# Ring of three in-place tiles for gates and z, and the late modulation's columns in the ring of the weights

## The chip, the cores and the metric

One NeuronCore of one Trainium2 chip runs one layer of a diffusion backbone in a single launch. The metric is device time in microseconds, the median of several runs of the whole program. Engines are named as in the profile: PE (TensorE, matmuls), PEld (its weight loads), DVE (VectorE), ACT (ScalarE), POOL (GpSimd), and SP (SyncE), which here only issues transfers.

## The reference, cut to what matters

256 latent tokens and 256 context tokens of width 2048 go through: a modulated RMS norm; one input projection that feeds latent attention (8 heads), a bidirectional gated DeltaNet (8 heads, chunks of 64) and two gates; the merge of both branches with sigmoid gates; one output projection; a second modulated norm; and a gated MLP of hidden width 5504 with a short convolution. Only the latent tokens are returned.

```
sh1, sc1, g1, sh2, sc2, g2 = split(silu(c) @ w_ada + b_ada, 6)
... split_columns(modulate(rmsnorm(x), sh1, sc1) @ w_in)
y_dn = rmsnorm(o, o_norm) * silu(z)
merged = sigmoid(gate_mla) * (y_mla @ w_o_mla) + sigmoid(gate_dn) * (y_dn @ w_o_dn)
x = x + g1 * (merged @ w_out)
x = x + g2 * conv_glu(modulate(rmsnorm(x), sh2, sc2), w_up, conv, w_down)
```

The first two parts of the modulation (`sh1`, `sc1`) are needed at once. The other four (`g1`, `sh2`, `sc2`, `g2`: 8192 columns of `w_ada`, 64 MB) are needed only from the output projection on: they are the late modulation of the title.

## The kernel before

**Layout and staging.** Activations lie transposed, channels on the 128 partitions, tokens along the free dimension (T = 256). Every large weight comes from HBM in pieces of 128 x 1024 f32 (512 KB) into a ring `raw` of NR = 4 slots (L105). `split` (L98 to L101) makes a high part on ACT (`whi`) and the rest on DVE (`wlo`), in halves of 512 columns with NH = 6 buffers each; `mm_hl` (L133) multiplies by the high part with 512 columns and by the low part with 256. So a piece of weights feeds 8 pairs of matmuls.

**Late modulation.** `ada_rest` (L222) goes through 16 blocks of 512 columns. For each it loads 16 tiles of 128 x 512 (256 KB) into a ring `rawa` of NA = 2 slots, one load ahead, and DVE adds each, times one entry of `sc` = silu(c), to `acc` (L238, L240): 256 loads and 256 multiplications in all. Ones-matmuls on PE then sum `acc` over the partitions into `adaT` (L246). It is a generator, driven by a `Side` object: other loops call `ada(ns)`, and it goes on until the budget is used, 650 ns for each step. The loop over DeltaNet heads gives it budget, then the attention, the scan, the output projection and the gated MLP. Before the second norm it is run until 12 blocks are done (L1207).

**Gates and z.** `gate_tiles` (L716) computes the 8 tiles of z (`wz`) and 2 x 16 of the gates (`wgm`, `wgd`) as fill work for PE under the attention and the scan. `gate_fin` (L707) brings a result into a tile `zx` (2 buffers), takes its tanh into a tile `zt` (1 buffer) and stores that to DRAM (L714). For z, `z_fin` (L728) multiplies on DVE first.

**Stages.** First norm and first projections; DeltaNet heads (`dn_head`); `inverse` (L628), a triangular inverse of 32 x 32 blocks that DVE computes in 30 steps (L642, L644), beside the projections `wkva` and `wqa`; then 32 small stores of its result to DRAM (L652 to L660); attention over 4 pairs of heads with z and gates as fill; the scan; merge, output projection, second norm (`h2_tile`, L1218) and gated MLP. At the start of attention the rotated key `krf` is copied to the other partitions by a DMA (L783) and cast to `krt`; `kps`, `ksq` and `ks` are the keys, their squares and their sums.

**What sets the order.** The code is traced in this order, but a list scheduler orders the instructions of each engine by its own estimates, with priority to what was traced first and once a slot is free. Every engine then runs its list in order. All transfers, loads and stores alike, are issued by SP in one list: one that waits for a slot or for data holds up all behind it.

Of the kernel before, what the change touches and what calls it, by code (L numbers as in the profile page):

```python
# [8 lines left out]
F32 = mybir.dt.float32  # L9
F32R = mybir.dt.float32r  # L10
AF = mybir.ActivationFunctionType
ALU = mybir.AluOpType
# [4 lines left out]
P = 128  # L17
D = 2048
KD = D // P
T = 256  # L20
# [6 lines left out]
G3 = 96 + 256 * N1  # L27
GR = 1024
GH = 512
NR = 4  # L30
NA = 2
NH = 6
AD = 0.45
GD0 = 2
# [20 lines left out]
def hybrid_block(ctx: ExitStack, tc: tile.TileContext, io, dbg=None):  # L55
    nc = tc.nc
    act, dve, pool, pe, sync = nc.scalar, nc.vector, nc.gpsimd, nc.tensor, nc.sync


    def pool_(name, bufs, side="left"):  # L60
        return tc.tile_pool(name=name, bufs=bufs, side=side, reuse_waits="tile")

    const = ctx.enter_context(pool_("const", 1))
    ad = ctx.enter_context(pool_("ad", 2))
    hp = ctx.enter_context(pool_("hp", 1))
    wr = ctx.enter_context(pool_("wr", 2))
# [17 lines left out]
    def vectors(pl, name, names):  # L84
        t = pl.tile([P, io[name].shape[1]], F32, name=name)
        sync.dma_start(t, io[name])
        pos, d = 0, {}
        for nm, n in names:
            d[nm] = t[:, pos : pos + n]
            pos += n  # L90
        return d

    off = vectors(const, "vecs", VECS)
# [9 lines left out]
    def raw_w(src):  # L103
        n = src.shape[1]
        raw = wr.tile([P, GR], F32, tag="raw", name="raw", bufs=NR)[:, :n]  # L105
        sync.dma_start(raw, src)
# [37 lines left out]
    def col_sum(out, x, w, start=True, stop=True):  # L144

        for j in range(4):
            js = slice(32 * j, 32 * j + 32)
            pe.matmul(out[js], x[:, js], w, start=start, stop=stop)
# [73 lines left out]
    def ada_rest():  # L222

        def load(i):
            w = ad.tile([P, 512], F32, tag="rawa", name="rawa", bufs=NA)
            b, q = divmod(i, 16)
            sync.dma_start(w, io["wada2"][b, q // 4, :, q % 4 * 512 : q % 4 * 512 + 512])
            return w

        ahead = [load(i) for i in range(NA - 1)]  # L230
        for b in range(16):
            acc = ad.tile([P, 512], F32, tag="acc", name="acc")
            for q in range(16):
                if 16 * b + q + NA - 1 < 256:
                    ahead.append(load(16 * b + q + NA - 1))
                w, c = ahead.pop(0), sc[:, q, 0:1]
                if q == 0:
                    dve.tensor_scalar(out=acc, in0=w, scalar1=c, scalar2=None, op0=ALU.mult)  # L238
                else:
                    dve.scalar_tensor_tensor(out=acc, in0=w, scalar=c, in1=acc, op0=ALU.mult, op1=ALU.add)  # L240
                if q < 15:
                    yield 650
            ps = psa.tile([P, 4], F32, tag="aux", name="adp")
            for j in range(4):
                col_sum(ps[:, j : j + 1], acc[:, j * P : (j + 1) * P], ones[:, 0:1])
            dve.tensor_tensor(out=adaT[:, 4 * b : 4 * b + 4], in0=ps, in1=bada[:, 32 + 4 * b : 36 + 4 * b], op=ALU.add)  # L246
            ada.done = b + 1
            yield 650
# [22 lines left out]
    sc = const.tile([P, KD, 2], F32, name="sc")  # L271
# [20 lines left out]
    def shift_mm(p):  # L292
# [3 lines left out]
        for m in range(4):  # L296
            raw = wr.tile([P, GR], F32, tag="raw", name="raw", bufs=NR)
            sync.dma_start(raw, io["wadab"][p, m])
# [79 lines left out]
    def gather(ps, M, out, scale=None):  # L378

        act.copy(out, ps[:M, T:])  # L380
        dve.tensor_tensor(out=out, in0=ps[:M, :T], in1=out, op=ALU.add)
# [49 lines left out]
    u = pg.tile([P, 8, 8], F32, name="ux")  # L431
# [48 lines left out]
    for st in range(8):  # L480
        B = [pg2.tile([P, 8, 64], F32R, tag=f"B{n}", name="B") for n in range(2)]
        for n in range(2):
            dve.tensor_tensor(out=B[n], in0=mle64.unsqueeze(1).broadcast_to([P, 8, 64]),
                              in1=ghl[:, n, st].unsqueeze(2).broadcast_to([P, 8, 64]), op=ALU.mult)
# [114 lines left out]
    def head_inputs(h):  # L599
# [13 lines left out]
        return xs[0], xs[1], xq  # L613

    ada = Side(ada_rest())
    ada.done = 0
    order = (0, 3, 1, 4, 2, 5, 6, 7)
# [84 lines left out]
    Ys = dram.tile([P, HEADS, T], F32, name="Ys")  # L702
    Zs = dram.tile([P, HEADS, T], F32, name="Zs")
    Gs = dram.tile([2, P, KD, T], F32, name="Gs")
    pz = ctx.enter_context(pool_("pz", 2))

    def gate_fin(ps, out, fin):  # L707
        x = pz.tile([P, T], F32, tag="zx", name="zx")
        gather(ps, P, x)
        t = pz.tile([P, T], F32, tag="zt", name="zt", bufs=1)  # L710
        act.activation(t, x, AF.Tanh, scale=0.5)
        if fin is not None:
            fin(x, t)
        sync.dma_start(out, t)  # L714

    def gate_tiles(jobs):  # L716

        for w, f, out, fin in jobs:
            W = lazy_w(io[w][f])
            ps = psm.tile([P, 512], F32, tag="mm", name="gtp")  # L720
            for k in range(KD):
                mm_hl(ps, P, W(k * P), H[0][:, k], k == 0, k == KD - 1)
                if k % 4 == 3 and k < KD - 1:
                    yield 1300
            gate_fin(ps, out, fin)
            yield 1300

    def z_fin(x, t):  # L728
        dve.scalar_tensor_tensor(out=t, in0=t, scalar=1.0, in1=x, op0=ALU.add, op1=ALU.mult)
        dve.tensor_scalar(out=t, in0=t, scalar1=off["o_norm"], scalar2=0.5, op0=ALU.mult, op1=ALU.mult)  # L730

    fill = Side(gate_tiles([("wz", f, Zs[:, f], z_fin) for f in range(HEADS)] + [("wgm", f, Gs[0, :, f], None) for f in range(KD)]))
    pC = ctx.enter_context(ExitStack())
    pc = pC.enter_context(pool_("pc", 1))
# [248 lines left out]
    for b in range(4):  # L983
        at, pr = mla_attend(b), mla_project(b + 1) if b < 3 else iter(())
        for n in range(7):
            for st in (pr, at):
                c = next(st, None)
# [256 lines left out]
    for f in range(NFF):  # L1244
        xs = []
        for w in ("wgate", "wval"):
# [6 lines left out]
            x = pf2.tile([P, T], F32, tag=w, name="fx")  # L1253
# [121 lines left out]
```

## Time and profile before

| | |
|---|---|
| three runs, median (lowest to highest) | 1940.28 us (1939.37 to 1945.17) |
| profiled execution: its time, its span | 1937.21 us, 1935.4 us |
| mean granted TensorE clock | 0.967 |
| DMA traffic over the span | 418.26 MB, mean 216 GB/s |
| share of the span with PE busy, DVE busy, ACT busy | 94%, 74%, 47% |

The span runs from the first to the last instruction of the profiled execution. Engine shares are averages over stages that are limited by different things, so the views by stretch of time, by waits and by line count for more. A wait in these views is idle time of an engine, put down to what ended it. In the prediction, 0 is the start of the span, and a line such as L240 is a line of the kernel before.

### The profile page before, as it was taken

To read this page: it belongs to the slowest core of one execution; us is meant where nothing else is said; L and a number is where in the kernel's file an instruction comes from. 1 tells how busy PE (TensorE), PEld (TensorE's weight loads), DVE (VectorE), ACT (ScalarE), POOL (GpSimd) and SP (SyncE) were. 2 spreads that over 40 slices of the span, in tenths; PEclk is the share of its full clock that TensorE was granted. 3 is DMA by queue.
4 is the path that set the end of the run, shared out by engine and by line. 5 is a ranking of instruction groups with operands and counts; after the bars stand their busy time and mean duration, and the time that the engine had idled before them with its cause. 6 is when DMAs were issued, how large, how long until landed. Compare 5 with 4: busy or idle time off the path is not lost.

```text
span 1935.4 us, 34978 instructions
## 1 busy us (share of the span) xinstructions
PE 1826.2 (94%) x13186; PEld 1552.7 (80%) x13186; DVE 1437.0 (74%) x2854; ACT 915.9 (47%) x1882; POOL 41.7 (2%) x45
## 2 busy tenths in 40 slices
PE   7889988999879999999999997999999999999999
PEld 5677867788678878778888885888888888888887
DVE  4998887777768778656679888887778777755554
ACT  3224443333367656543245545555554555544443
POOL 0000000000000000000000000000000000000000
PEclk7899988999889999999999998999999999999999
DMA  8984576665676777788776886776667565566664
GB/s 319 317 290 163 170 202 204 202 195 183 124 239 209 221 223 227 239 254 260 227 266 206 259 282 201 251 252 184 189 203 236 186 184 186 179 195 200 194 193 128
DMA packets 222521, 418.26 MB, mean 216 GB/s; under 512 B 71504, under 2 KB 113616, under 8 KB 219920
## 3 DMA queue, kind: packets, MB, share of 16 engines
q1 hardware_dynamic: 222352, 416.04, 69.1%
q8 instruction: 103, 1.69, 0.4%
q14 instruction: 66, 0.54, 0.1%
HBM read 387.00 MB, written 28.84 MB: 215 GB/s over the span
## 4 chain that ended last, share of the span: by engine, by line
PE 50%; issue 10%; DMA 6%; DVE 4%; ACT 1%; POOL 0%; SPq 0%; POOLq 0%; DVEq 0%; ACTq 0%
PE fps L141 13%; PE dps L141 8%; PE fps L142 7%; DMA rawa<-in_wada 5%; PE gtp L141 5%; PE dps L142 4%; PE gtp L142 2%; DVE acc L240 1%; DVE wlo L101 1%; PE brp L141 1%; PE kp L1084 1%; PE fps L139 1%; PE yp L1093 1%; DMA raw<-in_wgate 1%; PE op L1105 1%
## 5 line engine op out<-in xcount | busy, mean ns | idle before, releaser
L101 DVE TENSOR_TENSOR wlo<-raw,whi 128x512 fp32r<-128x512 f32 (+1 forms) x940 | 634.9, 685 | 197.4 <-ACT whi L100 186.2
L100 ACT CAST whi<-raw 128x512 fp32r<-128x512 f32 (+1 forms) x940 | 571.7, 618 | 415.5 <-PE dps L141 117.4
L141 PE MATMUL fps<-H,whi 128*128 128x512 f32 x1290 | 461.9, 399 | 5.8 <-DVE H L101 5.8
L142 PE MATMUL fps<-H,wlo 128*128 128x256 f32 x1290 | 363.7, 282 | 2.4 <-DVE wlo L101 2.4
L141 PEld LDWEIGHTS fps<-H,whi 128*128 128x128 f32 x1290 | 243.3, 189 | 62.3 <-DVE H L101 4.8
L142 PEld LDWEIGHTS fps<-H,wlo 128*128 128x128 f32 x1290 | 244.8, 190 | 7.7 <-DVE wlo L101 4.0
L240 DVE SCALAR_TENSOR_TENSOR acc<-rawa,sc,acc 128x512 f32<-128x512 f32 x240 | 179.2, 747 | 76.7 <-DMA rawa<-in_wada 75.4
L141 PE MATMUL mmp<-h,whi 128*128 128x512 f32 x600 | 225.2, 413 | 0.9 <-ACT whi L100 0.9
L141 PE MATMUL gtp<-h,whi 128*128 128x512 f32 x600 | 220.8, 404 | 0.0
L141 PE MATMUL dps<-GB,whi 128*128 128x512 f32 x544 | 193.0, 397 | 0.0
L142 PE MATMUL mmp<-h,wlo 128*128 128x256 f32 x600 | 174.8, 292 | 7.7 <-DVE wlo L101 7.7
L142 PE MATMUL gtp<-h,wlo 128*128 128x256 f32 x600 | 171.0, 285 | 0.0
L142 PE MATMUL dps<-GB,wlo 128*128 128x256 f32 x544 | 153.1, 282 | 0.0
L141 PEld LDWEIGHTS mmp<-h,whi 128*128 128x128 f32 x600 | 117.5, 196 | 27.7 <-ACT whi L100 1.3
L141 PEld LDWEIGHTS gtp<-h,whi 128*128 128x128 f32 x600 | 113.6, 189 | 25.8 <-issue 1.5
L142 PEld LDWEIGHTS mmp<-h,wlo 128*128 128x128 f32 x600 | 118.1, 197 | 10.2 <-DVE wlo L101 8.4
L141 PEld LDWEIGHTS dps<-GB,whi 128*128 128x128 f32 x544 | 102.1, 188 | 25.3
L142 PEld LDWEIGHTS gtp<-h,wlo 128*128 128x128 f32 x600 | 114.2, 190 | 4.2 <-issue 1.0
L142 PEld LDWEIGHTS dps<-GB,wlo 128*128 128x128 f32 x544 | 102.5, 188 | 0.0
L344 PE MATMUL fp<-h,gh 128*128 128x256 f32 (+1 forms) x224 | 60.9, 306 | 17.0 <-ACT h L335 17.0
L319 DVE CUSTOM_DVE_ANT_0 junk<-wt,scb 128x2048 bf16<-128x2048 f32 x32 | 73.1, 2284 | 0.1
L345 PE MATMUL fp<-h,gh 128*128 128x256 f32 (+1 forms) x224 | 65.9, 302 | 1.6 <-DVE h L336 1.4
(599 smaller groups left out, 2960.5 us busy)
## 6 DMA issues: line engine op xcount, KB each, us to landing
rawa<-in_wada SPq DMA_DIRECT2D x256, 256.0 KB, 4.0
raw<-in_wgate SPq DMA_DIRECT2D x82, 512.0 KB, 4.5
raw<-in_wval SPq DMA_DIRECT2D x82, 512.0 KB, 4.4
raw<-in_wdown SPq DMA_DIRECT2D x80, 512.0 KB, 4.3
wt<-in_wadas SPq DMA_DIRECT2D x16, 1024.0 KB, 7.4
raw<-in_wadab SPq DMA_DIRECT2D x32, 512.0 KB, 6.4
raw<-in_wgm SPq DMA_DIRECT2D x32, 512.0 KB, 4.7
raw<-in_wgd SPq DMA_DIRECT2D x32, 512.0 KB, 5.2
```

The costliest lines, as they stand in the source:

```text
L100: act.copy(hi, raw)
L101: dve.tensor_tensor(out=lo, in0=raw, in1=hi, op=ALU.subtract)
L139: pe.matmul(ps[:M, :], hi, xf, start=False, stop=True)
L141: pe.matmul(ps[:M, :], hi, xf, start=first, stop=False)
L142: pe.matmul(ps[:M, :T], lo, x[:, 0, :], start=False, stop=last)
L240: dve.scalar_tensor_tensor(out=acc, in0=w, scalar=c, in1=acc, op0=ALU.mult, op1=ALU.add)
L319: dve.tensor_tensor_reduce(out=junk, in0=w, in1=scb[:, s], scale=1.0, scalar=0.0, op0=ALU.mult, op1=ALU.add, accum_out=m[:, s : s + 1])
L344: pe.matmul(ps, hi, H[s][:, k, 0], start=k == 0 and s == 0, stop=False)
L345: pe.matmul(ps, hi, H[s][:, k, 1], start=False, stop=False)
L1084: pe.matmul(kp[hs, j], kt[:, h, hs], S[:, h, d], start=True, stop=True)
L1093: pe.matmul(yp[:, j], tt[:, 4 * q + j], rs[q][:, j], start=True, stop=True)
L1105: pe.matmul(op[q][:, j, d], S[:, h, d], qe[:, h, 64 * d : 64 * d + 64], start=False, stop=d == 1)
```

## The change

The tiles of the late modulation take slots of the ring `raw`, which has five now in place of four; the ring `rawa` is gone. A load brings 1024 columns, that is two of the former tiles, and DVE multiplies its halves one after the other; one load is issued ahead as before. A step of `ada_rest` still is one multiplication. The space is the same: four slots of 4 KB and two of 2 KB for each partition became five of 4 KB.

For gates and z, `zx` has three buffers and `zt` none of its own. The tanh of a gate is written over its input; for z the tanh takes a second tile of the same ring, and the product is written over the input. What is stored is `zx`.

```diff
-NR = 4
-NA = 2
+NR = 5
...
         def load(i):
-            w = ad.tile([P, 512], F32, tag="rawa", name="rawa", bufs=NA)
-            b, q = divmod(i, 16)
-            sync.dma_start(w, io["wada2"][b, q // 4, :, q % 4 * 512 : q % 4 * 512 + 512])
+            w = wr.tile([P, GR], F32, tag="raw", name="rawa", bufs=NR)
+            b, u = divmod(i, 8)
+            sync.dma_start(w, io["wada2"][b, u // 2, :, u % 2 * GR : u % 2 * GR + GR])
             return w
 
-        ahead = [load(i) for i in range(NA - 1)]
+        ahead = load(0)
         for b in range(16):
             acc = ad.tile([P, 512], F32, tag="acc", name="acc")
-            for q in range(16):
-                if 16 * b + q + NA - 1 < 256:
-                    ahead.append(load(16 * b + q + NA - 1))
-                w, c = ahead.pop(0), sc[:, q, 0:1]
-                if q == 0:
-                    dve.tensor_scalar(out=acc, in0=w, scalar1=c, scalar2=None, op0=ALU.mult)
-                else:
-                    dve.scalar_tensor_tensor(out=acc, in0=w, scalar=c, in1=acc, op0=ALU.mult, op1=ALU.add)
-                if q < 15:
-                    yield 650
+            for u in range(8):
+                w = ahead
+                if 8 * b + u < 127:
+                    ahead = load(8 * b + u + 1)
+                for q in range(2):
+                    c, wq = sc[:, 2 * u + q, 0:1], w[:, q * 512 : q * 512 + 512]
+                    if u + q == 0:
+                        dve.tensor_scalar(out=acc, in0=wq, scalar1=c, scalar2=None, op0=ALU.mult)
+                    else:
+                        dve.scalar_tensor_tensor(out=acc, in0=wq, scalar=c, in1=acc, op0=ALU.mult, op1=ALU.add)
+                    if u + q < 8:
+                        yield 650
...
-    pz = ctx.enter_context(pool_("pz", 2))
+    pz = ctx.enter_context(pool_("pz", 3))
 
     def gate_fin(ps, out, fin):
         x = pz.tile([P, T], F32, tag="zx", name="zx")
         gather(ps, P, x)
-        t = pz.tile([P, T], F32, tag="zt", name="zt", bufs=1)
-        act.activation(t, x, AF.Tanh, scale=0.5)
-        if fin is not None:
-            fin(x, t)
-        sync.dma_start(out, t)
+        if fin is None:
+            act.activation(x, x, AF.Tanh, scale=0.5)
+        else:
+            fin(x)
+        sync.dma_start(out, x)
...
-    def z_fin(x, t):
-        dve.scalar_tensor_tensor(out=t, in0=t, scalar=1.0, in1=x, op0=ALU.add, op1=ALU.mult)
-        dve.tensor_scalar(out=t, in0=t, scalar1=off["o_norm"], scalar2=0.5, op0=ALU.mult, op1=ALU.mult)
+    def z_fin(x):
+        t = pz.tile([P, T], F32, tag="zx", name="zt")
+        act.activation(t, x, AF.Tanh, scale=0.5)
+        dve.scalar_tensor_tensor(out=x, in0=t, scalar=1.0, in1=x, op0=ALU.add, op1=ALU.mult)
+        dve.tensor_scalar(out=x, in0=x, scalar1=off["o_norm"], scalar2=0.5, op0=ALU.mult, op1=ALU.mult)
```

**What moves.** Slots that come free at other times make the scheduler order the instructions differently. In the changed kernel line numbers of the same code are one lower up to the function `ada_rest`, one higher behind it, and three higher behind `z_fin`.

DVE in the middle of the inverse, before (`ux` holds the blocks of the inverse, `acc<-rawa` is a multiplication of the late modulation, `kvx` a result of `wkva`):

```order
L644 TENSOR_TENSOR ux<-ux 128x2x11x20
L240 SCALAR_TENSOR_TENSOR acc<-rawa,sc,acc 128x512
L642 TENSOR_TENSOR ux<-ux 128x456
L101 TENSOR_TENSOR wlo<-raw,whi 128x512
L644 TENSOR_TENSOR ux<-ux 128x2x12x19
L240 SCALAR_TENSOR_TENSOR acc<-rawa,sc,acc 128x512
L642 TENSOR_TENSOR ux<-ux 128x468
L240 SCALAR_TENSOR_TENSOR acc<-rawa,sc,acc 128x512
L644 TENSOR_TENSOR ux<-ux 128x2x13x18
```

The same steps of the inverse on DVE now:

```order
L645 TENSOR_TENSOR ux<-ux 128x2x11x20
L100 TENSOR_TENSOR wlo<-raw,whi 128x512
L643 TENSOR_TENSOR ux<-ux 128x456
L645 TENSOR_TENSOR ux<-ux 128x2x12x19
L100 TENSOR_TENSOR wlo<-raw,whi 128x512
L643 TENSOR_TENSOR ux<-ux 128x468
L645 TENSOR_TENSOR ux<-ux 128x2x13x18
```

No multiplication of the late modulation stands within the inverse now, where there were 7 from its first to its last step; of the splits of weights 18 stand there, where there were 23.

SP at the end of the burst of small stores, before (the last four stores of the inverse's result, L653 to L660, and what follows; `wz`, `wkvb` and `wqb` are weights of z and of the attention):

```order
L653 DMA Xd<-ux 32x32x32
L658 DMA Xs<-ux 16x32x32 x4
L660 DMA Xs<-ux 32x16x32 x2
L714 DMA Zs<-zt 128x256
L783 DMA krf<-krf 64x512
L677 DMA xd<-Xd 128x2x128
L106 DMA raw<-in_wkvb 128x1024
L106 DMA raw<-in_wz 128x1024
L714 DMA Zs<-zt 128x256
```

The same place on SP now:

```order
L654 DMA Xd<-ux 32x32x32
L659 DMA Xs<-ux 16x32x32 x4
L661 DMA Xs<-ux 32x16x32 x2
L715 DMA Zs<-zx 128x256
L786 DMA krf<-krf 64x512
L105 DMA raw<-in_wz 128x1024
L678 DMA xd<-Xd 128x2x128
L226 DMA rawa<-in_wada 128x1024
L105 DMA raw<-in_wz 128x1024
L226 DMA rawa<-in_wada 128x1024
L105 DMA raw<-in_wkvb 128x1024
```

Ahead of the burst stand, after the first load of `wkvb`, three loads of `wz` before and one now; the other two and two loads of the modulation stand between `krf` and the second load of `wkvb`.

DVE at the second norm, before (`x` is the sum of input and mixer, `bc_ps` its inverse root mean square, `h` and `H` the normed tiles and their low parts):

```order
L1220 TENSOR_TENSOR h_13567<-bc_ps,x_12429 128x256
L1220 TENSOR_TENSOR h_13580<-bc_ps,x_12429 128x256
L246 TENSOR_TENSOR adaT<-adp,vecs 128x4
L240 SCALAR_TENSOR_TENSOR acc<-rawa,sc,acc 128x512
L101 TENSOR_TENSOR H_13538<-h_13567,H_13538 128x256
L101 TENSOR_TENSOR H_13538<-h_13580,H_13538 128x256
L1220 TENSOR_TENSOR h_13593<-bc_ps,x_12429 128x256
L1220 TENSOR_TENSOR h_13606<-bc_ps,x_12429 128x256
L240 SCALAR_TENSOR_TENSOR acc<-rawa,sc,acc 128x512 x2
L101 TENSOR_TENSOR H_13538<-h_13593,H_13538 128x256
```

The same steps on DVE now:

```order
L1223 TENSOR_TENSOR h_13343<-bc_ps,x_12227 128x256
L1223 TENSOR_TENSOR h_13356<-bc_ps,x_12227 128x256
L100 TENSOR_TENSOR H_13314<-h_13343,H_13314 128x256
L100 TENSOR_TENSOR H_13314<-h_13356,H_13314 128x256
L1223 TENSOR_TENSOR h_13369<-bc_ps,x_12227 128x256
L1223 TENSOR_TENSOR h_13382<-bc_ps,x_12227 128x256
L100 TENSOR_TENSOR H_13314<-h_13369,H_13314 128x256
```

Between the last `x1` and the first result of the gated MLP 14 multiplications stood on DVE, and two stand there now; the two that stood between `x` and the sum of squares (L1200 and L1204) are gone. In the scan there are 34 instead of 17, and behind the second norm 59 instead of 36.

## The prediction

> **What bounds the kernel now.** I read the page first: how much of the span TensorE (PE) is busy, and what its chain holds.
>
> ```profile
> span 1935.4 us, 34978 instructions
> PE 1826.2 (94%) x13186; PEld 1552.7 (80%) x13186; DVE 1437.0 (74%) x2854; ACT 915.9 (47%) x1882; POOL 41.7 (2%) x45
> PE 50%; issue 10%; DMA 6%; DVE 4%; ACT 1%; POOL 0%; SPq 0%; POOLq 0%; DVEq 0%; ACTq 0%
> ```
>
> PE is the bound over the whole: 109 us of the span (1935.4 - 1826.2) are not PE. Matmul work does not change here, so a gain can only come out of those 109 us and out of matmuls that run at a lowered clock behind a gap. An average over stages says little, so the second view is busy time by stretch.
>
> ```profile
> core 0: us, PE busy (x) PEld busy (x) DVE busy (x) ACT busy (x) POOL busy (x), PEclk, DMA share, GB/s
> 446.00:508.00 62.00, 53.39 (x434) 45.06 (x433) 54.97 (x114) 24.33 (x50) 2.34 (x3) 0.86 0.47 141
> 508.00:530.00 22.00, 21.32 (x155) 17.27 (x154) 12.80 (x32) 8.58 (x18) 0.81 (x1) 1.00 0.79 118
> 530.00:546.00 16.00, 4.92 (x81) 4.35 (x80) 6.23 (x14) 6.66 (x13) 1.33 (x1) 0.59 0.89 236
> 546.00:800.00 254.00, 243.68 (x1899) 210.86 (x1898) 198.18 (x421) 161.80 (x378) 12.66 (x11) 0.99 0.72 222
> 1066.00:1178.00 112.00, 108.58 (x668) 92.69 (x666) 95.10 (x183) 55.61 (x118) 0.00 (x0) 1.00 0.82 265
> 1178.00:1217.00 39.00, 25.18 (x171) 20.51 (x164) 31.74 (x72) 22.66 (x49) 0.70 (x1) 0.82 0.65 203
> ```
>
> The first two columns are the stretch and its length. Three stretches lose most: 446 to 508 (the triangular inverse on VectorE, DVE, which is busy 55 of 62 us), 530 to 546 (PE nearly still, clock 0.59) and 1178 to 1217 (the second norm, PE busy 25 of 39). Between 546 and 800 PE loses 10 of 254.
>
> Third, what the modulation costs. Its loads are the largest DMA wait of DVE; the two lower rows give the median from issue to landing of a load of each size.
>
> ```profile
> DVE acc L240 <- DMA rawa<-in_wada: 75.4, 78, 3.0
> rawa<-in_wada SPq DMA_DIRECT2D x256, 256.0 KB, 4.0
> raw<-in_wgate SPq DMA_DIRECT2D x82, 512.0 KB, 4.5
> ```
>
> 75 us over 78 waits, but DVE is not the bound everywhere: such a wait counts only where PE waits behind it.
>
> **The change, part by part.** *Arithmetic:* the 256 multiplications of the modulation stay, on the same shape; two tanh forms and the two z operations stay too. Nothing is priced there. 128 DMA issues fewer on SP's queue, and a load of double size lands in about 4.5 instead of 4.0 us, so two multiplications wait for 4.5 where they waited for 8. That this is hidden or not is settled stage by stage.
>
> *Inverse and the store burst (446 to 546).* This chain carries most.
>
> ```profile
> 446.35 0.21 DVE L642 TENSOR_TENSOR ux<-ux 128x60 f32<-128x60 f32 x1
> 505.93 0.27 DVE L644 TENSOR_TENSOR ux<-ux 128x60 f32<-128x60 f32 x1
> 509.32 0.33 SPq L652 DMA_DIRECT2D Xd<-xt  x1
> 534.60 0.54 SPq L783 DMA_DIRECT2D krf<-krf  x1
> 536.31 0.42 ACT L711 ACTIVATE zt<-zx 128x256 f32<-128x256 f32 x1 [8.27 <-DMA Zs<-zt]
> 536.92 0.62 ACT L100 CAST krt<-krf 128x512 fp32r<-128x512 f32 x1 [0.20 <-DMA krf<-krf]
> 541.52 0.61 PE L148 MATMUL ks<-ones,ksq 128*32 128x1 f32 x32 [11.08 <-ACT ksq L827]
> ```
>
> DVE works through the inverse from 446 to 506; the 32 stores of X follow on SP from 509 to 534; the small stores and `krf` stand behind them. PE's longest gap, 11.08 us, is at the end of this. The ring of three takes away the 8.27 us for which the single `zt` buffer held ScalarE (ACT) until its store had landed. **It gives almost nothing here:** the cast of `krt` is next but one on ACT in the changed order too, and it waits for `krf`, issued at 534.60. In the row it became free 0.20 us after the tanh. So I price that edit at 0 to 0.2 us.
>
> What does move the end of that chain is the DVE work inside the inverse.
>
> ```profile
> L101 DVE TENSOR_TENSOR wlo<-raw,whi 128x512 fp32r<-128x512 f32 x23 | 15.7, 685 | 0.0
> L240 DVE SCALAR_TENSOR_TENSOR acc<-rawa,sc,acc 128x512 f32<-128x512 f32 x7 | 5.2, 747 | 3.4 <-DMA rawa<-in_wada 3.4
> 526.05 0.40 PE L141 MATMUL gtp<-h,whi 128*128 128x512 f32 x1
> 526.41 0.40 PE L141 MATMUL gtp<-h,whi 128*128 128x512 f32 x1
> ```
>
> Seven multiplications stand in it, 5.2 us with 3.4 us of waiting; in the changed order none does. Five of its 23 weight splits fall behind its end: 5 x 0.685 = 3.4 us. Together 5.2 + 3.4 + 3.4 = 12.0 us by which the stores can start earlier. Against it: two loads of `wz` that stood ahead of the burst now stand behind it on SP. Each feeds 8 pairs of matmuls, and a pair takes 0.35 to 0.36 us (526.05 to 526.41): 2 x 8 x 0.35 = 5.6 us of PE work that can no longer fill the burst. The split work that falls behind the inverse goes into the burst, where DVE is busy 13 of 22 us. Net 12.0 - 5.6 = **-6.4 us**; bounds -12.0 (PE finds other work) and +5.6 (the inverse ends no sooner).
>
> *The late attention (546 to 800).*
>
> ```profile
> PE rps L896 <- ACT qx L863: 4.6, 3, 2.9
> DVE acc L240 <- DMA rawa<-in_wada: 31.3, 34, 3.0
> 701.31 0.75 DVE L240 SCALAR_TENSOR_TENSOR acc<-rawa,sc,acc 128x512 f32<-128x512 f32 x1 [2.70 <-DMA rawa<-in_wada]
> 704.42 1.22 PE L896 MATMUL rps<-qx,rope 128*128 128x256 f32 x2 [2.90 <-ACT qx L863]
> ```
>
> DVE waits 31.3 us for these loads, but PE loses only 254.00 - 243.68 = 10.3 us, the 4.6 of the first row included. The two last rows are one event: 2.70 us on DVE become 2.90 us on PE, since DVE finishes `qx` behind the wait. With half the loads I take away half of the 31.3, and of PE's 10.3 I take 4: **-4 us**, bounds 0 and -10.3. DVE's other saving is hidden by the fill matmuls of `wz` and `wgm`; where PE has no idle time, it is worth nothing.
>
> *The second norm (1178 to 1217).*
>
> ```profile
> PE ss L148 <- DVE ssq L1204: 6.3, 1, 6.3
> PE fps L141 <- DVE H L101: 5.8, 5, 2.3
> L240 DVE SCALAR_TENSOR_TENSOR acc<-rawa,sc,acc x13: 739/751/753, 1183.2 to 1217.8; 128x512 f32<-128x512 f32 x13
> 1183.17 0.75 DVE L240 SCALAR_TENSOR_TENSOR acc<-rawa,sc,acc 128x512 f32<-128x512 f32 x1
> ```
>
> DVE makes the tiles of H on which PE waits, and 13 multiplications stand between them (13 x 0.75 = 9.8 us); in the changed order there are two. Those between `x1` and `ssq` cost at most one 0.75 plus one 0.48, partly under the square on ACT. I take 3.3 of the 5.8 and 0.7 of the 6.3: **-4 us**; bounds 0 and -7 (5.8 + 1.2).
>
> *The last loads (1440 to 1500) and the rest.*
>
> ```profile
> PE fps L142 <- DVE wlo L101: 1.8, 2, 1.1
> ```
>
> These 1.8 us stand behind waits for the modulation; its work is spread over more of the gated MLP now: **-1 us**, bounds -3 and +3, the upper for the scan (800 to 1000), which gets 34 multiplications instead of 17. DVE has room there (139 of 216 us busy from 800 to 1016 on the same view), and PE waits for little. From 1300 on PE is full. A weight load feeds 8 pairs, 2.8 us. If the modulation holds two of the five slots, three are left, a round of 8.4 us, in which a load lands (4.5 us) and is split twice (1.4 us on DVE, and the casts before it); so I price that at nothing. Without that cover each late load costs its lateness.
>
> *A rule weighed.* Row first: the granted clock from 530 to 546 is 0.59. The Trainium skill, page "TensorE: Matmul & The Clock Gate", section "Part 1: The HAM clock gate", says that an idle window of about 3.4 us halves the clock and about as long a busy stretch restores it. By that rule a gap that shrinks but stays above 3.4 us saves none of the ramp. Both large gaps stay above it in my sum, so I add nothing; had they gone below it, an estimate from the page's 3.4 us at half speed is 1.7 us more for each, and the sum would be 3.4 us lower. The trace agrees with the rule's direction.
>
> **Sum.** -6.4 - 4 - 4 - 1 = -15.4 us. The profiled execution took 1937.21 us (span 1935.4), so it would take 1921.8. The runs shown have their median at 1940.28, 3.07 above it: 1924.9, say **1925 us**.
>
> **The rivals.** *No change:* the stall moves only. For it: `krf` is late next, the stores of X also wait for ACT and PE, and in 546 to 800 PE is busy 96%. If the inverse gains just the 5.6 us that the two loads cost, and half of the other terms is hidden, the time is 1940 - 4 = 1936, within 5.8 us (0.3%, about what a measurement of this kernel can tell from no change). Against it: DVE's 12 us are on a serial chain that SP waits for.
>
> *Slower, by the shared queue:* behind the burst the second `wkvb` load, which stood third after `Zs`, stands behind two loads of `wz` and two of the modulation. SP issues in order, so one modulation load that waits for a slot holds the attention's weights. Four loads of 0.5 MB at 236 GB/s (530 to 546) are 2.2 us each, 9 us in all. That decides once the inverse ends less than 9 us earlier: with +9 there and the other terms at 0 the time is 1949. Against it: PE has 16 pairs of `gtp` to do meanwhile, 5.6 us.
>
> *Larger:* if DVE really paced 546 to 800, all 10.3 us of PE go and the inverse gives its 12.0: -12 - 10.3 - 7 - 3 = -32, 1908.
>
> *It doesn't do what it says:* the ring of three frees nothing as priced above; this is in the forecast already.
>
> **Chances.** Forecast, 1914 to 1934: 0.62. Larger: 0.11. No change: 0.15. Slower: 0.12. So faster by over 0.3% is 0.73, within it 0.15, slower 0.12. The range is 1908 to 1941: the low end is the sum of the bounds, the high one takes in no change and leaves out most of the slower case.
>
> **What would show it.** The first store of X about 12 us sooner after the first row of the inverse; the gap before `ks` still there and above 3.4 us, ended by `krf` or the `wz` load and no longer by a `Zs` store; DVE's waits for `rawa` near half of 75 us; the waits for H between 1178 and 1217 at half. Wrong would be: weights (`whi` on ACT) waiting for DMA in the attention, or SP held for modulation slots longer than now.

## The result, and the profile after

The changed kernel takes **1919.19 us** (median of 6 runs, 1911.35 to 1928.57) where the kernel before takes 1940.88 (6 runs): a ratio of 0.990, 95% interval 0.988 to 0.992. It is faster, inside the range and 5.8 us below the forecast. The profiled executions differ by 14.7 us (1937.21 and 1922.51; forecast 15.4). The profiled run of before lies 3.7 us below its median and that of the changed kernel 3.3 us above its own, so the medians are further apart than the traces; the traces tell where some 15 us went. (A few executions of the experiments were in a slow state, the first profiled one without waits among them, at a granted clock of 0.60; the ratios leave them out and no trace of one is read.)

The page of the changed kernel, the same rows as before:

```profile
span 1920.4 us, 34673 instructions
PE 1820.5 (95%) x13186; PEld 1550.8 (81%) x13186; DVE 1438.2 (75%) x2854; ACT 922.1 (48%) x1882; POOL 43.1 (2%) x45
PE 76%; issue 10%; DVE 8%; DMA 3%; ACT 1%; SPq 1%; POOL 1%; POOLq 0%; ACTq 0%; DVEq 0%
```

TensorE (PE) works 5.7 us less and idles 9.3 us less (1935.4 - 1826.2 = 109.2, now 1920.4 - 1820.5 = 99.9). The matmul count is the same and the mean granted clock is 0.970 where it was 0.967, so the matmuls took less time because they ran at a higher clock.

For a ledger I cut both traces at the same events: the first `U` of DeltaNet, first and last step of the inverse (446.35 and 505.93 before), first `ks`, first matmul of the scan, its last update of the state (`sp_`), first and last `ops` of the output projection, first `fps` of the gated MLP, and its last part. Busy time by stretch, the kernel before (columns as in the prediction):

```profile
226.70:446.35 219.65, 201.59 (x1746) 167.76 (x1745) 170.77 (x354) 85.82 (x177) 14.19 (x14) 0.93 0.71 205
446.35:505.93 59.58, 50.97 (x420) 42.95 (x419) 53.66 (x111) 22.62 (x48) 2.34 (x3) 0.86 0.46 135
505.93:541.52 35.59, 23.83 (x169) 19.21 (x167) 16.94 (x41) 13.12 (x26) 0.81 (x1) 0.88 0.81 152
541.52:827.70 286.18, 275.10 (x2176) 238.29 (x2176) 214.10 (x448) 179.31 (x411) 16.73 (x15) 0.98 0.74 227
...
965.90:1081.80 115.90, 113.56 (x794) 96.79 (x793) 100.57 (x230) 61.00 (x131) 2.90 (x1) 0.99 0.73 235
1081.80:1177.30 95.50, 92.08 (x545) 78.50 (x543) 78.73 (x146) 45.51 (x95) 0.00 (x0) 1.00 0.83 270
1177.30:1190.50 13.20, 2.89 (x86) 1.95 (x84) 9.44 (x25) 4.24 (x10) 0.70 (x1) 0.66 0.58 188
1190.50:1688.30 497.80, 491.87 (x2849) 425.21 (x2850) 389.70 (x760) 270.47 (x541) 0.00 (x0) 1.00 0.65 205
```

The same view of the changed kernel, cut at the same events:

```profile
231.90:448.00 216.10, 194.22 (x1731) 161.46 (x1732) 168.32 (x350) 87.25 (x180) 15.04 (x14) 0.95 0.70 207
448.00:498.60 50.60, 47.49 (x420) 39.98 (x419) 47.25 (x100) 22.22 (x48) 2.32 (x3) 0.98 0.33 102
498.60:540.00 41.40, 29.26 (x181) 23.36 (x180) 22.08 (x49) 15.43 (x29) 0.69 (x1) 0.82 0.82 178
540.00:813.90 273.90, 271.84 (x2193) 236.84 (x2192) 211.72 (x445) 181.56 (x414) 17.31 (x15) 1.00 0.75 235
...
952.00:1071.30 119.30, 114.52 (x795) 97.13 (x794) 100.94 (x230) 62.25 (x133) 2.89 (x1) 0.99 0.69 227
1071.30:1167.40 96.10, 93.07 (x545) 80.65 (x543) 74.44 (x139) 48.39 (x97) 0.00 (x0) 0.96 0.75 247
1167.40:1176.30 8.90, 1.98 (x54) 1.24 (x52) 4.81 (x16) 3.00 (x7) 0.69 (x1) 0.75 0.29 90
1176.30:1673.20 496.90, 493.54 (x2880) 427.42 (x2881) 398.55 (x777) 273.83 (x541) 0.00 (x0) 0.99 0.67 214
```

Length after minus length before:

| stretch | change, us | in the forecast |
|---|---|---|
| start and DeltaNet, up to the inverse | +5.2 - 3.5 = +1.7 | 0 |
| the inverse | -9.0 | -12.0 |
| from its end to the first `ks` | +5.8 | +5.6 |
| attention, up to the scan | -12.3 | -4 |
| scan; from its end to the first `ops`; `ops` | -0.1; +3.4; +0.6 | 0 |
| second norm | -4.3 | -4 |
| gated MLP | -0.9 | -1 |
| sum | -15.1 | -15.4 |

The sum agrees; the rows for the inverse, the attention and the parts that I had at 0 do not. The waits that answer to those of the prediction, over the whole changed kernel and then in the attention alone (before: 75.4 us in 78 waits, and 31.3 in 34):

```profile
DVE acc L241 <- DMA rawa<-in_wada: 32.7, 28, 5.8
...
DVE acc L241 <- DMA rawa<-in_wada: 8.4, 11, 1.8
...
PE rps L899 <- ACT qx L866: 1.3, 2, 0.9
```

The first is a little under half, as forecast; in the attention they fell by 23 us, far more than half. The 4.6 us of `rps`, the wait of 2.90 us among them, are down to 1.3 us.

### The profile page after: what moved, and what is told of

It reads as the page before. It is cut to its first block, busy times and chain, and to the rows that moved or that the text cites. A ratio compares the mean times of both kernels' runs of the same rounds, so it can differ in the third digit from the quotient of the medians.

```text
span 1920.4 us, 34673 instructions
## 1 busy us (share of the span) xinstructions
PE 1820.5 (95%) x13186; PEld 1550.8 (81%) x13186; DVE 1438.2 (75%) x2854; ACT 922.1 (48%) x1882; POOL 43.1 (2%) x45
## 4 chain that ended last, share of the span: by engine, by line
PE 76%; issue 10%; DVE 8%; DMA 3%; ACT 1%; SPq 1%; POOL 1%; POOLq 0%; ACTq 0%; DVEq 0%
PE fps L140 16%; PE dps L140 8%; PE fps L141 8%; PE gtp L140 6%; PE mmp L140 6%; PE dps L141 4%; PE gtp L141 3%; PE mmp L141 3%; DVE junk L320 3%; PE brp L140 1%; PE fps L138 1%; PE fp L346 1%; PE kp L1087 1%; PE fp L345 1%; PE fp L347 1%
## 5 line engine op out<-in xcount | busy, mean ns | idle before, releaser
L140 PE MATMUL mmp<-h,whi 128*128 128x512 f32 x600 | 217.2, 401 | 2.7 <-ACT whi L99 2.7
L241 DVE SCALAR_TENSOR_TENSOR acc<-rawa,sc,acc 128x512 f32<-128x512 f32 x240 | 179.1, 746 | 34.6 <-DMA rawa<-in_wada 32.7
L141 PE MATMUL mmp<-h,wlo 128*128 128x256 f32 x600 | 170.5, 286 | 7.9 <-DVE wlo L100 7.9
L140 PEld LDWEIGHTS mmp<-h,whi 128*128 128x128 f32 x600 | 113.3, 189 | 27.9 <-ACT whi L99 3.0
L141 PEld LDWEIGHTS mmp<-h,wlo 128*128 128x128 f32 x600 | 113.8, 190 | 11.3 <-DVE wlo L100 9.6
```

Source lines behind the costliest of these rows:

```text
L140: pe.matmul(ps[:M, :], hi, xf, start=first, stop=False)
L141: pe.matmul(ps[:M, :T], lo, x[:, 0, :], start=False, stop=last)
L241: dve.scalar_tensor_tensor(out=acc, in0=wq, scalar=c, in1=acc, op0=ALU.mult, op1=ALU.add)
```

## The experiments

All times are medians; the ratio is to the kernel before, run beside it on the same chip (its medians there: 1940.21, 1938.46 and 1938.74 us). VectorE is DVE, SyncE is SP, ScalarE is ACT, GpSimd is POOL.

| kernel | modulation's loads | weight slots | us | ratio, 95% interval |
|---|---|---|---|---|
| before | 512, own ring of 2 | 4 | 1940 | 1 |
| changed | 1024, shared | 5 shared | 1919.2 | 0.988 to 0.992 |
| ring of three alone | 512, own 2 | 4 | 1943.6 | 1.0001 to 1.003 |
| modulation alone | 1024, shared | 5 shared | 1922.5 | 0.989 to 0.994 |
| shared, 512 | 512, shared | 5 shared | 1937.3 | 0.996 to 0.999 |
| own ring, 1024 | 1024, own 2 | 3 | 1938.0 | 0.996 to 1.0004 |
| three slots | 512, own 2 | 3 | 1959.8 | 1.008 to 1.013 |
| four shared slots | 1024, shared | 4 shared | 1953.7 | 1.005 to 1.009 |
| own ring, 512 deep | 512, own 4 | 3 | 1922.2 | 0.989 to 0.994 |

### One part alone

The ring of three on the kernel before (the hunks at `pz`, `gate_fin` and `z_fin` alone).

> The kernel before with only the ring of three in place for the gate and z tiles; the modulation as before (own ring of two 512-wide tiles, four weight slots). Theory (the prediction): 0 to -0.2 us, ratio 0.999 to 1.001, since the cast of krt waits for krf next; the gap before ks stays at 10 to 11 us and is ended through krf. Rival (the ring of three frees ScalarE): the gap shrinks by up to 8.3 us, ratio near 0.996.

Ratio 1.002, interval 1.0001 to 1.003: nothing gained. Here is ScalarE ahead of the attention in this kernel (start, duration, instruction, and in brackets the idle time before it and what ended it):

```profile
527.37 0.42 ACT L730 ACTIVATE zt<-zx 128x256 f32<-128x256 f32 x1 [0.49 <-DVE zx L381]
536.75 0.62 ACT L100 CAST krt<-krf 128x512 fp32r<-128x512 f32 x1 [8.96 <-DMA krf<-krf]
```

The tanh runs 9 us sooner than before (536.31 there); the 8.27 us wait for the store of `zt` is gone, and 8.96 us for `krf` stand in its place. The step of the prediction is seen in two rows. That PE's gap was 14.19 us here, and not 10 to 11, is the expectation's miss: it ended with a late `wkvb` load.

The other part alone, which is the changed kernel with the old gate and z tiles:

> The changed kernel with the gate and z tiles as before (two zx, one zt): only the modulation's columns go through the ring of the weights, five slots, 1024 per load. Theory: all of the gain, 1919 to 1925 us, ratio 0.988 to 0.992. Rival (the ring of three has a part of it): 1927 to 1933, ratio 0.993 to 0.996.

0.991, interval 0.989 to 0.994, beside 0.988 to 0.992 with both parts: the whole gain within the error. The profiled execution has the same ledger: 239.2 us from the first `ks` to the last `s_` (239.4 in the changed kernel), inverse 50.6 in both.

### Load size, ring or slot

```
-            w = ad.tile([P, 512], F32, tag="rawa", name="rawa", bufs=NA)
+            w = wr.tile([P, GR], F32, tag="raw", name="rawa", bufs=NR)[:, :512]
```

> The kernel before with the modulation's loads left at 512 wide (256 loads) but put into the ring of the weights, five slots. No multiplication stands in the inverse now, as in the changed kernel. Theory (width halves the waits): only the inverse's term is left, -6 us, ratio near 0.997; VectorE still waits about 75 us for rawa. Rival (sharing the ring does it: it moves the multiplications and shortens no load): -15 to -20 us, ratio 0.990 to 0.992.

0.998: the inverse's term and no more, as expected. The inverse takes 50.8 us in its trace, as in the changed kernel, with no multiplication in it. DVE's waits for `rawa` are 57 us, nearer to 75 than to 33. Its attention up to the scan takes 289.8 us, no less than before (286.2). (Its profiled execution is its fastest, 15 us under its median, so I read no total from it.) So sharing the ring moves the multiplications, and that alone is worth about 3 us (1 to 8 by the interval).

The reverse, 1024 per load in a ring of its own; only three weight slots fit beside it:

```
-            w = wr.tile([P, GR], F32, tag="raw", name="rawa", bufs=NR)
+            w = ad.tile([P, GR], F32, tag="rawa", name="rawa", bufs=2)
```

> The modulation's loads 1024 wide (128 loads) in a ring of their own with two tiles; to fit in memory the weights keep three slots. Gate and z tiles as before. Eight multiplications stand in the inverse. Theory (width): the terms of the late attention and the second norm are left, -8 us, less what the lost weight slot costs (0 to 8): ratio 0.996 to 1.000, and VectorE's waits for rawa near 38 us. Rival (sharing the ring does it): nothing gained, ratio 1.000 to 1.005, by the lost slot.

0.998 again, at the middle of the theory's range; waits for `rawa` 32.5 us. The attention up to the scan takes 272.7 us (273.9 in the changed kernel): that gain does not need the shared ring. But the scan takes 150.9 us and not 138.2. To price the lost slot by itself, the kernel before with `NR = 3`:

> The kernel before with three weight slots in place of four and nothing else: the price of a weight slot, which the own ring of 1024-wide tiles had to give up. Theory (that price swallowed the own ring's gain): 8 to 15 us slower, ratio 1.004 to 1.008, most of it in the scan (800 to 970), where the own ring lost 12.7 us. Rival (the slot is free, a wide load on its own gains nothing): ratio 1.000 to 1.002.

1959.8 us, 1.010: some 20 us, above both ranges, and not mainly in the scan (+5.2 there); the output projection has +8.1 and the gated MLP +7.8. Against this kernel the 1024-wide ring gains 1959.8 - 1938.0 = 22 us at equal weight slots, but with 4 KB more of memory per partition for the modulation.

Then the slot count in the shared ring, the modulation alone with `NR = 4`:

> The modulation alone through the ring of the weights at 1024 per load, as in the changed kernel, but with four slots and not five (gate and z tiles as before). Theory: a modulation tile takes the fourth slot most of the time, so this pays about what the loss of a weight slot costs: 1925 to 1935 us, ratio 0.992 to 0.998. Rival (the fifth slot does nothing): 1920 to 1924, ratio 0.989 to 0.992.

1953.7 us, 31 us slower than with five slots and slower than before. Both guesses were too kind. Here the waits of DVE for `rawa` are back at 68 us, and the scan takes 155.6 us. The prediction's "nothing" for the ring holds for five slots and would have been wrong for four.

### How much the waits cost at most

The kernel before with its loads, but the multiplications read a tile that never changes:

```
+        fixed = ident.unsqueeze(1).broadcast_to([P, 4, P])
...
-                    dve.scalar_tensor_tensor(out=acc, in0=w, scalar=c, in1=acc, op0=ALU.mult, op1=ALU.add)
+                    dve.scalar_tensor_tensor(out=acc.rearrange("p (a b) -> p a b", a=4), in0=fixed, scalar=c, in1=acc.rearrange("p (a b) -> p a b", a=4), op0=ALU.mult, op1=ALU.add)
```

> The kernel before with all its loads of the modulation, but the multiplications read one fixed tile, so VectorE never waits for rawa (the modulation's values are not the reference's); two multiplications stand in the inverse, not seven. It bounds what the 75 us of waits cost. Theory (the waits pace the late attention, more than the 4 us that the prediction took): 20 to 30 us faster, ratio 0.985 to 0.990, the stretch from the first ks to the last s_ 14 us shorter or more. Rival (PE hides the waits and the gain is the queue's): the inverse's term and little else, 5 to 8 us, ratio 0.996 to 0.998.

> The kernel whose modulation multiplies a fixed tile while its loads go on, once more, for a profile of it at full clock: its first profile was taken at a granted clock of 0.60, and its time was 43 us below before. Theory (the waits pace every stage that interleaves the modulation with weight splits): the gain is spread, 5 us or more each in DeltaNet (227 to 446), the late attention, wout with the second norm, and the gated MLP. Rival (the late attention alone): 25 us or more of it between the first ks and the last s_.

1896.89 us: 0.978, interval 0.976 to 0.980, more than either theory said. The second run (one execution, 1897.22 us) gave the trace. Its DeltaNet stage, from the first `U` to the inverse:

```profile
224.10:418.80 194.70, 190.78 (x1740) 159.65 (x1741) 170.56 (x352) 85.44 (x176) 13.60 (x14) 1.00 0.82 237
```

219.65 us before, 194.70 here, the clock at 1.00 where it was 0.93: 25 of the 40 us that the traces differ by lie in a stage for which the prediction had no term. The output projection with the second norm gives 10.7 (95.5 + 13.2 before, 89.2 + 8.8 here), the gated MLP 4.2 and the attention up to the scan only 2. Two stretches are longer than before: the one from the inverse to the first `ks` by 10.5 us and the scan by 12.4. They and the attention in this kernel:

```profile
470.10:516.20 46.10, 31.72 (x177) 25.65 (x175) 20.23 (x45) 16.14 (x30) 1.02 (x1) 0.75 0.81 176
516.20:800.30 284.10, 273.26 (x2177) 238.02 (x2176) 209.43 (x438) 179.14 (x407) 17.56 (x15) 0.98 0.80 248
800.30:950.90 150.60, 148.44 (x1121) 122.01 (x1120) 108.94 (x262) 53.28 (x108) 0.00 (x0) 1.00 0.74 239
```

Two of the theory's four stages gave 5 us or more; the theory is half right, and the rival is wrong. In the attention PE idles 10.8 us, as before, though no multiplication waits. Other waits stand there:

```profile
PE yp L1094 <- DMA jit<-Xs: 4.9, 1, 4.9
PE rps L897 <- ACT qx L864: 4.6, 1, 4.6
732.49 0.62 ACT L100 CAST whi<-raw 128x512 fp32r<-128x512 f32 x1 [5.91 <-DMA raw<-in_wgm]
```

The second stands behind the third, a weight load that came late. So this kernel changes which loads come when, and is no clean bound for a single stage. The kernel also cuts a second wait: a load needs no slot that a multiplication still reads. DVE itself waits directly for `rawa` for only 3.9 us in this stage before, so those 25 us are not DVE's own waits for data; SP's waits for slots do not account for them alone either (the last section has the rows). Multiplications stand elsewhere too: 32 of them ahead of the first `U` where there were 14; in the DeltaNet stage itself there are no fewer than before (46, and 42 before). What made the 25 us, and how the 40 us split between the two waits and this order, stays open.

### The gap ahead of the attention

In the changed kernel PE stands still for 11.88 us. Rows of SP, ACT and PE around it:

```profile
498.89 0.33 SPq L654 DMA_DIRECT2D Xd<-ux  x1
525.89 0.54 SPq L786 DMA_DIRECT2D krf<-krf  x1
526.47 0.57 SPq L105 DMA_DIRECT2D raw<-in_wz  x1
528.21 0.62 ACT L99 CAST krt<-krf 128x512 fp32r<-128x512 f32 x1 [13.96 <-DMA krf<-krf]
530.86 1.14 ACT L99 CAST whi<-raw 128x512 fp32r<-128x512 f32 x2 [1.54 <-DMA raw<-in_wz]
531.53 0.80 PE L140 MATMUL gtp<-h,whi 128*128 128x512 f32 x1 [11.88 <-ACT whi L99]
```

The stores of X begin at 498.89, and SP issues `krf` and the next `wz` load at their end. Two kernels tried to take this gap away. First, the 32 stores on GpSimd's queue (`sync.dma_start` of the stores in `inverse` becomes `pool.dma_start`):

> The changed kernel with the inverse's 32 stores of X issued on GpSimd's queue and not on SyncE's. Theory (the gap of 11.9 us ahead of the attention is SP's queue held by the stores, with krf and the wz load behind them): the gap falls to 2 to 5 us and the kernel gains 6 to 10 us on the changed one, 1909 to 1914 us, ratio 0.984 to 0.987. Rival (the 16 DMA engines, not the queue, hold the loads, or GpSimd issues more slowly): 1917 to 1922, ratio 0.988 to 0.991, the gap above 9 us.

1931.1 us, 0.995 (0.993 to 0.997): some 10 to 12 us slower than the changed kernel, outside both ranges. GpSimd also computes the power in the norms, and there is one in this stretch:

```profile
528.23 1.29 POOL L661 DMA_DIRECT2D Xs<-ux  x2
529.53 0.72 POOL L151 TENSOR_TENSOR ms<-ms,half 128x2 f32<-128x2 f32 x1
```

Its input was ready at 504.4 (the last DVE operation on `ms`); it ran behind the last store at 529.53. DVE took up the result only at 548.2 (from 496 to 562 it waited 19.3 us for `rawa`), and PE waited 12.05 us for it. The queue was free, and the gap was as long as in the changed kernel (11.88 us).

Second, the block from `cosT, sinT, perm` to the cast of `krt` moved ahead of the query projection, so that SP issues `krf` at 485.7:

> The changed kernel with the rotated keys (krf, its copy across partitions and the cast of krt) computed ahead of the query projection, so that the copy is issued ahead of the store burst. Theory (the gap of 11.9 us is ended by the wz load behind the burst): the gap shrinks by 0 to 2 us, 1916 to 1920 us, ratio 0.988 to 0.991. Rival (krf holds ScalarE and that is the gap): it falls to about 3 us, 1909 to 1913, ratio 0.984 to 0.987.

1920.9 us, 0.991: no change against the changed kernel. The longest gap is 8.78 us now, 3.1 less and not 0 to 2, and it is ended by the `wz` load; `ks` starts earlier, but the attention has the work that waited. So `krf` accounts for no more than 3.1 us of the gap, and what is left ends with the weights behind the burst; what the gap would be without them, no run shows.

### Depth

Two loads ahead instead of one in the changed kernel (`ahead = [load(0), load(1)]`, and each step issues the load after next):

> The changed kernel with two loads of the modulation ahead in the ring of five instead of one. Theory (a slot of the weights is worth more than the waits that are left): two to three of five slots go to the modulation, 1925 to 1945 us, ratio 0.993 to 1.003. Rival (the 33 us of waits that are left still pace VectorE): 1905 to 1914, ratio 0.983 to 0.988, waits for rawa below 15 us.

1922.1 us, 0.992 (0.990 to 0.994): neither theory by the median, though the interval reaches into the first one's range. The waits for `rawa` did not fall (37.4 us, and 10.9 in front of the first multiplications of a block; 32.7 and 4.1 in the changed kernel), and no price of a slot is seen beyond the error. In a shared ring a load that is issued earlier waits for the slot that is next in turn, so being written earlier need not mean being loaded earlier; that is argued, not shown.

And the kernel before with `NR = 3`, `NA = 4`: loads of 512, three ahead in a ring of their own.

> The modulation 512 wide in an own ring of four tiles, three loads ahead, with three weight slots: the same memory as the own ring of two 1024-wide tiles, which took 1938 us where three slots with the ring of before took 1960. Theory (what counts is how many columns are on the way): 1936 to 1944 us, ratio 0.998 to 1.003. Rival (the number of loads counts, each with its own landing time): 1952 to 1960, ratio 1.007 to 1.011.

1922.2 us, 0.991 (0.989 to 0.994): better than the theory, and equal to the changed kernel within the error. It has small loads, 256 of them, three weight slots, the old z tiles, and 8 multiplications in the inverse. The wait for the modulation in this kernel:

```profile
DVE acc L240 <- DMA rawa<-in_wada: 14.6, 18, 2.4
```

14.6 us and not 75.4. So the number of loads is not what counts, nor is the shared ring. It reaches that time by other stages, though: beside the attention (273.5 us) it gains 12 us in DeltaNet (207.6) and only 3 in the inverse (56.2), and its scan is 5.6 us longer (143.8). In the same memory, four tiles of 512 beat two of 1024 by 16 us (1922.2 and 1938.0): a tile of 1024 comes free only after two multiplications, and one load is on the way; of the four small ones three are. Of the kernels that use the modulation's loads, none beats the changed one by more than the error.

## Why the prediction was right, point by point

**The ring of three, priced at a gain of 0 to 0.2 us: shown.** Alone it gives nothing, and the wait for `krf` stands where the wait for the store stood.

**Inverse and burst, forecast -6.4, measured -9.0 + 5.8 = -3.2.** The first store comes 12.0 us sooner after the first row of the inverse (509.32 - 446.35 = 62.97, now 498.89 - 447.96 = 50.93), just as forecast, of which 3.1 us lie behind the inverse's last row. The term mis-sized is the price of the two `wz` loads behind the burst. Their 16 pairs run from 531.53 to the first `ks` at 540.00, 8.5 us and not 5.6, since the clock was at 0.50 behind the gap until about 537:

```profile
531.50:536.00 4.50, 4.47 (x13) 3.55 (x14) 3.96 (x7) 2.61 (x5) 0.00 (x0) 0.50 1.00 358
536.00:540.00 4.00, 4.00 (x21) 3.27 (x20) 3.62 (x8) 2.23 (x5) 0.00 (x0) 0.87 0.83 328
```

I priced a pair from rows at full clock, next to a gap that I had kept. That multiplications inside the inverse are worth little is also shown by the experiments: with 512 shared they are gone for 3 us in all, and the deep ring has eight, with an inverse of 56.2 us, and is as fast over the whole.

**The late attention, forecast -4, measured -12.3: the step that failed.** Two things in the sentence "With half the loads I take away half of the 31.3, and of PE's 10.3 I take 4" were wrong. The waits fell by 23 us and not by 16, and PE's idle time up to the scan fell from 11.1 to 2.1 us: 9 us of it went with these waits, where I had taken 4 of 10.3. The other kernels bear this out, one excepted. The stretch from the first `ks` to the scan in each trace:

| kernel | DVE's waits for `rawa` there, us | PE idle, us | length, us |
|---|---|---|---|
| ring of three alone | 34.7 | 12.0 | 286.3 |
| before | 31.3 | 11.1 | 286.2 |
| shared, 512 | 29.9 | 10.6 | 289.8 |
| three slots | 28.3 | 11.2 | 284.3 |
| four shared slots | 18.7 | 7.8 | 277.0 |
| own ring, 1024 | 18.6 | 6.3 | 272.7 |
| two loads ahead | 14.3 | 2.1 | 274.3 |
| modulation alone | 11.1 | 1.9 | 273.6 |
| changed | 8.4 | 2.1 | 273.9 |
| own ring, 512 deep | 7.0 | 2.1 | 273.5 |

The kernel without waits is the exception (0, 10.8 and 284.1), behind the other waits shown above. (With `krf` early, and with the stores on GpSimd, the stretch begins at another point of the work, so they are not in the table.) And a wait costs more than its length, which is the second thing. These are the stretches behind the 2.90 us wait that the prediction quoted, in the kernel before:

```profile
704.40:706.00 1.60, 1.58 (x34) 0.93 (x38) 0.93 (x3) 0.44 (x1) 0.00 (x0) 0.50 0.85 314
706.00:708.00 2.00, 2.00 (x37) 1.79 (x31) 2.00 (x6) 0.00 (x0) 0.00 (x0) 0.50 0.97 291
708.00:710.00 2.00, 2.00 (x8) 1.71 (x8) 1.10 (x3) 1.33 (x3) 1.11 (x1) 0.50 0.71 259
```

The clock stood at 0.50 for at least 5.6 us behind it: another 2.8 us of work lost, an estimate at half speed. From 700 to 750 the granted clock was 0.93 before and is 1.00 now. A second such ramp moved: before, it lay behind the first `ks`, now it is paid ahead of it, within the 8.5 us above.

```profile
541.50:546.00 4.50, 4.48 (x78) 4.23 (x79) 3.07 (x9) 3.50 (x7) 1.33 (x1) 0.50 0.96 345
```

The two ramps are more than the 3.3 us by which PE's busy time fell; against them the changed kernel does about eight more pairs of fill matmuls in this stretch (376 `gtp` by the low part, 367 before). So -10.3 was no bound: it counted idle time and left out the clock. The width alone gives this term too (272.7 us with the own ring of 1024), and sharing alone does not (289.8 us with 512 shared).

**Second norm, forecast -4, measured -4.3, by another way.** PE's waits between the last `ops` and the first matmuls of the MLP, changed kernel:

```profile
PE fps L140 <- DVE H L100: 5.8, 3, 2.9
PE ss L147 <- DVE ssq L1207: 2.6, 1, 2.6
```

I expected 3.3 us from H and 0.7 from `ssq`. The waits for H are 5.8 us as before, in three pieces and not five; `ssq` gave 3.7 us (6.3 before). What I had looked at ahead of `ssq` were the multiplications alone, one 0.75 and one 0.48. In the trace of before, DVE also has three splits of weights between the last `ops` and the last `ssq`, with 1.4 us of waits for their casts; in the changed kernel one split stands there. The neighbours moved, not only the modulation; that the size came out right is luck.

**What the sum owes to luck.** Inverse and attention gave -15.5 and not -10.4; start, DeltaNet and the stretches from the scan to the output projection, which I had at 0 with bounds of 3, gave back +5.6. One piece is seen, a new wait of PE of 2.2 us at 952, behind the scan, for a cast whose `wgd` load came late. Another is a wait of 3.03 us in the output projection of the changed kernel, behind DVE's longest wait for `rawa`:

```profile
1143.64 0.75 DVE L241 SCALAR_TENSOR_TENSOR acc<-rawa,sc,acc 128x512 f32<-128x512 f32 x1 [5.80 <-DMA rawa<-in_wada]
1145.38 0.58 PE L141 MATMUL ops<-MB,wlo 128*128 128x256 f32 x1 [3.03 <-DVE wlo L100]
1147.00:1149.00 2.00, 2.00 (x9) 1.71 (x8) 1.97 (x5) 0.92 (x3) 0.00 (x0) 0.50 0.87 276
1149.00:1151.00 2.00, 2.00 (x8) 1.71 (x8) 1.19 (x3) 1.05 (x4) 0.00 (x0) 0.50 1.01 378
```

The 33 us of waits that are left thus still cost TensorE time in places. What made the rest stays open. The step to the medians (+3.07 on the profiled time) assumed that the profiled run of the changed kernel would lie as far below its median as that of before did; it lay above.

**The rivals.** No change and slower by the shared queue did not come: behind the burst the modulation's loads delay nothing by 9 us. Yet with one slot less the shared ring does cost more than it gains: with four shared slots the kernel is slower than before. *Larger* had the attention right, where all of PE's 10.3 us went and more, and the other terms too large. One sign of being wrong did come: casts of weights on ACT wait 8.1 us for DMA in the attention (4.7 for `wz`, 1.9 for `wgd`, 1.5 for `wkvb`), where none did before; it did not outweigh the rest.

## What to carry to other kernels

Count what a ring has on the way, not only how many loads it takes: the same memory cut finer (four tiles of 512, three ahead) did what wider loads did for the whole time here. Before a second stream enters a ring of weights, price one slot by itself, here 20 us from four to three and 31 from five shared to four. And price a wait of a few us on TensorE with the slow matmuls behind it, about twice its length here.

## What the runs showed of the hardware

- **A wait of 2.90 us halved the clock, and so did one of 3.03 us.** The Trainium skill, page "TensorE: Matmul & The Clock Gate", section "Part 1: The HAM clock gate", puts the idle window at about 3.4 us; here PE's last matmul before the wait ended at 701.52, the next began at 704.42, and the clock, at 1.00 from 698 to 701, read 0.50 behind it. The measurement is shorter, so a gap under 3.4 us is not safe in this trace. The wait of 3.03 us in the changed kernel did the same (rows above). One of 2.22 us there left the clock at 1.00:

```profile
954.53 0.49 PE L140 MATMUL gtp<-h,whi 128*128 128x512 f32 x1 [2.22 <-ACT whi L99]
952.50:955.00 2.50, 0.47 (x1) 0.19 (x1) 0.49 (x1) 1.14 (x2) 0.00 (x0) 1.00 1.00 401
955.00:957.00 2.00, 1.77 (x11) 1.57 (x11) 1.97 (x4) 0.60 (x2) 0.00 (x0) 1.00 0.22 84
```

- **SP's waits at the loads of the modulation.** The largest group of that line over the whole kernel before, and over the changed kernel:

```profile
SPq L227 <- DMA rawa<-in_wada: 126.3, 83, 6.4
SPq L226 <- DVE wlo L100: 124.6, 58, 16.8
```

The names differ because in the shared ring a slot is mostly freed by a split of weights. All groups of the line together are 359.7 us before, 215.3 in the changed kernel and 256.0 without DVE's waits. SP issues in order, so weights stand behind each such wait. In the DeltaNet stage these sums are 63.9, 26.9 and 33.8 us, while the stage takes 219.7, 216.1 and 194.7. SP's waits fell most where the stage gained little, so they alone do not explain the 25 us.
